# Loading the first norm's scales alone, splitting the first weight loads, and moving one more projection ahead of the first norm in a streaming encoder step

## The chip, the cores and the metric

The kernel runs on one core of one Trainium2 chip. The metric is the device time of one execution in microseconds. The times before are those of three runs: 1094.95, 1096.83 and 1100.05 us, so the median is 1096.83 us. One execution was profiled apart; it took 1095.87 us and its recorded span is 1093.7 us.

## The reference, cut to what matters

One layer of a hybrid encoder works on 576 rows of width 1024: 512 rows of a prompt and 64 rows of a sample. The two are independent sequences with their own states; they share the weights.

```python
def _trunk(x, mem_k, mem_v, conv_a_prev, s_gdn, s_gla, ffn_prev, p):
    y, c_new, sa, sb = _mixer(_rmsnorm(x, p['norm_mix'][l]), p, l, ...)
    x = x + y
    x = x + _cross_attn(_rmsnorm(x, p['norm_mem'][l]), mem_k[l], mem_v[l], ...)
    f, f_new = _conv_ffn(_rmsnorm(x, p['norm_ffn'][l]), p['w_up'][l], ...)
    x = x + f
    return _rmsnorm(x, p['norm_final']), ...
```

`_mixer` projects the normalised rows to q, k and v of a gated delta rule (four heads, after a causal convolution of width 4), to q, k and v of a gated linear attention, to their gates and to two merge gates; both recurrences run in chunks of 64. `_conv_ffn` projects up to 2 x 2816 columns, convolves them causally (width 3), multiplies SiLU of one half with the other and projects down. Everything is float32; the states and the last rows before each convolution are outputs too.

## The kernel before, in words

The rows lie transposed: eight tiles `x[k]` of 128 features by 576 rows. Each float32 operand of a large product is split in a rounded part and a remainder (`xh`, `xl`; a weight tile gives `wh`, `wl`), and a product is the sum of three matmuls: `wh`·`xh`, `wh`·`xl`, `wl`·`xh`. One weight tile of 128 output columns (1024 floats per partition) makes two PSUM accumulators, of 256 and 320 rows: 48 matmuls. In a trace the weight loads are `wr<-wt` (on the queue of SyncE, SP), the split is two ACT instructions, and the remainder of most tiles is finished by a second load from DRAM that adds (`w<-wt`, issued by GpSimd, POOL).

The norm does not come first. The scale of the norm over features (`g`) is put into `xh`/`xl` by `norm_prep`, and the factor of each row (`rbc`) is applied when a PSUM result is taken out. So the projections start as soon as the first rows and weights are there, and the sums of squares (`ssq` in `c_rstat`), the reciprocal root (on POOL) and the broadcast of the factor (two `dg` tiles against ones) are worked out beside them.

What sets the order. All engine work is recorded by a planner, the class `Driver`. A main generator, `main`, yields the large projections tile by tile; smaller generators, called chains (convolutions, gates, the recurrences, the norms), are advanced between its pieces. The planner has a cost for each instruction and a time at which each tile is written; when a chain yields, its next piece may be put into TensorE's order only `MARGIN` us of planned time after its inputs are planned to be ready (`advance`, and `drain` where the main generator must wait). Instructions of ACT, DVE, POOL and SP come into their queues in the order of their planned starts. Each engine works its queue strictly in order, so an instruction that waits holds up everything behind it on that engine.

The beginning (lines 703 to 717 and `main` from line 1648): the loads of the vector table `vec` (276 columns), then alternately a tile of `x` and a piece of 512 columns of the first two weight tiles; on ACT and DVE the splits in the same order; then 96 matmuls for q and k of head 0 (`first2`). Behind these stand the sums of squares (20 small matmuls, `sm<-keep,acc` and `sm<-keep,sq`), 16 small products of `x` with the 32 columns of the low-rank gate (`sm<-x,w`), and then v of head 0. Its accumulators are taken out when the row factor is there; the chain `c_first` does that for q and k and starts the gates. The `HEADS` list then gives the order of the other projections, qb (the linear attention's q) next.

Further back: the merge gates (`gate_finish`, product form `run_product`) follow the recurrences; then `mem_prep` loads the sample's last rows of the ConvFFN (`fst`, DMA `fst<-st_ffn`) and the memory tokens (`mem`), whose squares are summed on POOL into `macc`; then eight `out` tiles. In the ConvFFN each of the 44 column tiles `fu` gets four small POOL instructions: a zero for the two columns ahead of the prompt, a copy of two columns from `fst` ahead of the sample, and two copies into `fout`.

Of the kernel before, what the change touches and what calls it, by code (L numbers as in the profile page):

```python
# [34 lines left out]
BACK = 6.0  # L35
MARGIN = 0.6
LAG = 0.0
NWARM = 18

# [221 lines left out]
class Driver:  # L261
# [7 lines left out]
    def __init__(self, pe, sync):  # L269
        self.pe, self.sync = pe, sync  # L270
        self.chains = []
        self.done = set()
        self.now = 0.0
        self.half = self.mode = None
        self.last = 0.0
        self.wrote = {}
# [185 lines left out]
    def drain(self, until):  # L462
        while not until():
            r = self.step(MARGIN)
            if r is None:
# [16 lines left out]
def tile_trunk(ctx, tc, xT, memT, wt, wd, vec, cst, w0, wgate, st_gdn, st_conv, st_gla, st_ffn, ckT, cv,  # L482
# [220 lines left out]
    cst_t = tp.tile([P, NM - 256], F32, tag="cst", name="cst", bufs=1)  # L703
    DMA(vec_t, vec)
    x = []
# [33 lines left out]
    V.tensor_scalar(onh, vcol(C_ONA, 2), 0.5, None, op0=ALU.mult)  # L739
    fst = cp.tile([P, 2 * NJ, 2], F32, name="fst")  # L740
    fout = cp.tile([P, 2 * NJ, 4], F32, name="fout")
# [67 lines left out]
    def ssq(accs, t, n, ps):  # L809

        for i, (acc, o) in enumerate(accs):
            PE.matmul(ps[0:n, t:t + 1], acc[:, o + t * 128:o + t * 128 + n], ones[:, 0:1], start=i == 0, stop=i == len(accs) - 1)

    def pads(t_):
# [827 lines left out]
    def main():  # L1642
# [4 lines left out]

        def wpart(i, k):
            c = slice(512 * k, 512 * k + 512)
            wh, wl = wready[i]  # L1650
# [25 lines left out]
        V.tensor_tensor(r4(w0_t, 32), r4(w0_t, 32), vcol(C_GMIX, 8).unsqueeze(2).broadcast_to([P, 8, 32]), op=ALU.mult)  # L1676
# [7 lines left out]
        drop(*(t_[:] for t_ in raws))  # L1684
        emit_weight(2)
        DMA(wg_t, wgate)
# [49 lines left out]
        for kd, i in HEADS:  # L1736
# [4 lines left out]
            elif kd == "qb":  # L1741
                drv.spawn(c_gla(i))
            b = b0
            if i > 0 or kd not in ("q", "k", "v"):
                b = []
# [68 lines left out]
        for pair, prod in product_order(GPAIRS):  # L1814
# [198 lines left out]
        def kept(col, u):  # L2013
            G.tensor_copy(fout[:, col, 0:2], u[:, 512:514])
            G.tensor_copy(fout[:, col, 2:4], u[:, 578:580])

# [3 lines left out]
        def scaled(j, col, u):  # L2020
            X.tensor_tensor(u[:, 2:582], u[:, 2:582], N["n3"][1][:, 0:580], op=ALU.mult)
            G.tensor_copy(u[:, 514:516], fst[:, col, :])
            kept(col, u)

        def up_finish(pair, prod, a, b, c):
            j = pair[0][1]
            if prod == "P1":
                ups[j] = slot("fu"), slot("fu")
                for u in ups[j]:
                    G.memset(u[:, 0:2], 0.0)  # L2030
            ug, uv = ups[j]
# [253 lines left out]
    def mem_prep():  # L2285
        DMA(fst, st_ffn)
        mxs = []
# [137 lines left out]
```

## Time and profile before

| what | us | where |
|---|---|---|
| median of three runs | 1096.83 | the times |
| profiled execution, its own time | 1095.87 | the times |
| span of that execution | 1093.7 | page |
| TensorE busy | 1081.5 | page, part 1 |
| DVE, ACT, POOL busy | 740.1, 707.9, 328.1 | page, part 1 |
| TensorE's share of the chain that ended last | 95% | page, part 4 |
| first large matmul | 6.65 | timeline |

A busy TensorE in this profile is not TensorE at its peak: matmuls overlap and their ends are modelled, so what a stretch is worth is read from the starts of its matmuls. Two groups of tile names matter: `bank` are the accumulators of the large products, `sm` those of the chains. The granted clock in the windows view is a share of full speed; records of it begin only 10.2 us into the span, so an earlier window shows 1.00 whatever it was.

### The profile page before, as it was taken

The numbers are of one execution on the slowest core, as the hardware profiler recorded it, in microseconds if no ns is written. First come the engines' busy times: TensorE is split into PE (matmuls) and PEld (weight loads), VectorE is DVE, ScalarE is ACT, GpSimd is POOL, SyncE is SP. The second block draws the span as 40 slices with busy tenths as digits, with TensorE's granted clock in tenths as the row PEclk, the third lists the DMA queues.
The fourth block names the chain that finished last, engine by engine and source line by source line (L and its number), as shares of the span: only waits on it lengthen the run. The fifth ranks groups of instructions, "written<-read, shape, count | busy, mean of one in ns | idle before, by whom it ended". The sixth has DMA issues, their size and how long they took to land.

```text
span 1093.7 us, 21490 instructions
## 1 busy us (share of the span) xinstructions
PE 1081.5 (99%) x8259; PEld 1048.5 (96%) x8259; DVE 740.1 (68%) x1446; ACT 707.9 (65%) x1385; POOL 328.1 (30%) x608
## 2 busy tenths in 40 slices
PE   9999999999999999999999999999999999999997
PEld 8999989998988999999999999999999999999997
DVE  6675647666676767977736768577796776676634
ACT  7766446754766786466756668866786675767643
POOL 2333014421432324022111122444443433434320
PEclk9999999999999999999999999999999999999999
DMA  8675235743556899488884359766887886787863
GB/s 266 135 174 121 39 82 119 182 100 88 124 112 148 196 231 221 170 226 203 226 211 129 70 125 228 176 148 125 187 185 184 178 201 147 181 190 168 171 120 111
DMA packets 67094, 174.88 MB, mean 160 GB/s; under 512 B 7664, under 2 KB 13168, under 8 KB 66992
## 3 DMA queue, kind: packets, MB, share of 16 engines
q0 software_dynamic: 30528, 73.41, 39.0%
q1 hardware_dynamic: 36464, 100.10, 28.7%
q8 instruction: 65, 1.06, 0.4%
q14 instruction: 37, 0.30, 0.1%
HBM read 159.99 MB, written 5.37 MB: 151 GB/s over the span
## 4 chain that ended last, share of the span: by engine, by line
PE 95%; DMA 2%; issue 2%; POOL 0%; ACT 0%; DVE 0%; DVEq 0%; POOLq 0%; SPq 0%
PE bank L292 65%; PE sm L292 30%; DMA wr<-wt 1%; DMA w<-ws 1%; DMA w<-wt 1%; POOL w L292 0%; ACT w L292 0%; DVE ws L292 0%; DVEq L2415 0%; POOL rtf L292 0%; SPq L292 0%; POOLq L2415 0%; ACT vb L292 0%; DVE rin L292 0%; POOLq L292 0%
## 5 line engine op out<-in xcount | busy, mean ns | idle before, releaser
L292 PE MATMUL bank<-xh,w 128*128 128x320 f32 (+3 forms) x1824 | 349.2, 303 | 1.8 <-ACT w L292 1.6
L292 PEld LDWEIGHTS bank<-xh,w 128*128 128x128 f32 x1824 | 279.2, 190 | 6.9 <-ACT w L292 1.7
L292 PE MATMUL bank<-ach,w 128*128 128x288 f32 (+3 forms) x1320 | 255.7, 296 | 1.2 <-DMA w<-ws 1.1
L292 POOL DMA_DIRECT2D w<-wt x149 | 131.5, 886 | 374.1 <-ACT w L292 319.3
L292 PEld LDWEIGHTS bank<-ach,w 128*128 128x128 f32 x1320 | 207.5, 188 | 2.6 <-DMA w<-ws 1.6
L292 PE MATMUL bank<-xl,w 128*128 128x256 f32 (+3 forms) x912 | 204.4, 296 | 0.0
L292 ACT CAST w<-wr 128x512 fp32r<-128x512 f32 (+2 forms) x201 | 158.3, 790 | 25.1 <-PE bank L292 14.8
L292 ACT ACTIVATE w<-wr 128x512 fp32r<-128x512 f32 (+2 forms) x181 | 142.8, 790 | 40.3 <-PE bank L292 29.3
L292 PE MATMUL bank<-acl,w 128*128 128x288 f32 (+3 forms) x660 | 159.2, 295 | 0.0
L292 PEld LDWEIGHTS bank<-xl,w 128*128 128x128 f32 x912 | 156.0, 190 | 0.0
L292 PE MATMUL sm<-ach,w 128*128 128x290 f32 (+1 forms) x576 | 124.6, 296 | 0.1
L292 PEld LDWEIGHTS bank<-acl,w 128*128 128x128 f32 x660 | 116.7, 188 | 0.0
L292 PEld LDWEIGHTS sm<-ach,w 128*128 128x128 f32 x576 | 95.7, 189 | 0.3 <-ACT kvh L292 0.3
L292 ACT CAST w<-ws 128x512 fp32r<-128x512 f32 x124 | 74.3, 615 | 26.5 <-DVE ws L292 17.4
L292 PE MATMUL sm<-acl,w 128*128 128x290 f32 (+1 forms) x288 | 79.1, 296 | 0.0
L292 DVE SCALAR_TENSOR_TENSOR fc<-fu,vec,fc 128x578 f32<-128x578 f32 x88 | 72.1, 829 | 9.7 <-ACT fc L292 9.5
L292 DVE TENSOR_TENSOR w<-ws,w 128x512 fp32r<-128x512 f32 x92 | 63.0, 688 | 16.7 <-ACT w L292 15.2
L292 DVE TENSOR_TENSOR x<-x,bank 128x256 f32<-128x256 f32 (+1 forms) x78 | 31.9, 443 | 38.9 <-PE bank L292 38.9
L292 PEld LDWEIGHTS sm<-acl,w 128*128 128x128 f32 x288 | 54.3, 189 | 0.0
L292 ACT ACTIVATE fc<-fu,vec 128x578 f32<-128x578 f32 x44 | 38.2, 871 | 24.1 <-POOL fu L292 24.0
L292 POOL DMA_DIRECT2D w<-wd x32 | 27.6, 873 | 82.7 <-ACT w L292 80.5
L292 PE MATMUL bank<-oh,w 128*128 128x256 f32 (+1 forms) x256 | 44.9, 295 | 0.3 <-DMA w<-wt 0.3
(381 smaller groups left out, 2008.0 us busy)
## 6 DMA issues: line engine op xcount, KB each, us to landing
wr<-wt SPq DMA_DIRECT2D x134, 512.0 KB, 5.7
w<-wt POOLq DMA_DIRECT2D x56, 512.0 KB, 7.3
w<-wt POOLq DMA_DIRECT2D x93, 256.0 KB, 6.0
wr<-wd SPq DMA_DIRECT2D x24, 384.0 KB, 4.1
w<-wd POOLq DMA_DIRECT2D x24, 384.0 KB, 6.6
w<-ws POOLq DMA_DIRECT2D x31, 256.0 KB, 4.6
x<-xT SPq DMA_DIRECT2D x16, 288.0 KB, 3.8
y<-xT SPq DMA_DIRECT2D x8, 288.0 KB, 4.3
```

The lines of the kernel that those rows point to most:

```text
L292: fn(*args, **kw)
```

## The change

It has five parts.

1. The eight columns of the first norm's scales are loaded alone in front; the other 268 columns of `vec` follow after the fourth `x` tile. What reads those other columns at the beginning (`ea` on ACT, `onh` on DVE) stands later in its queue.
2. The first two weight tiles are loaded and split in pieces of 256, 256 and 512 columns each (`FIRST`) in place of 512 and 512. The third weight tile is loaded and split earlier (`emit_weight(2)` before the squares).
3. The sums of squares of the first norm and the small products of `x` are placed by the planner inside v of head 0 and no longer ahead of it, and qb's first tile goes ahead of the wait for the first norm: q, k, v and qb, four tiles. The accumulators of q and k are taken out by ACT or DVE, whichever is planned to be free sooner (`moved`); it becomes DVE.
4. The chain margin is 0.3 up to the end of the merge gates and 0.6 behind (`drv.margin`).
5. `fst` is allocated late, with four columns per tile, the first two of them zero, so that one strided copy replaces the zero and the copy ahead of the sample, and one strided copy replaces the two into `fout` (`ends`).

```diff
-MARGIN = 0.6
+MARGIN = 0.3, 0.6
+FIRST = [(0, slice(0, 256)), (1, slice(0, 256)), (0, slice(256, 512)), (1, slice(256, 512)), (0, slice(512, 1024)), (1, slice(512, 1024))]
...
-            c[0] = self.last + MARGIN
+            c[0] = self.last + self.margin
         elif isinstance(r, list):
-            c[0] = self.ready_at(*r) + MARGIN
+            c[0] = self.ready_at(*r) + self.margin
...
-    DMA(vec_t, vec)
+    DMA(vec_t[:, C_GMIX:C_GMIX + KT], vec[:, C_GMIX:C_GMIX + KT])
...
-        if k < 4:
-            c = slice(512 * (k // 2), 512 * (k // 2) + 512)
-            DMA(raws[k % 2][:, c], wt[k % 2][:, c])
+        if k < 6:
+            a, c = FIRST[k]
+            DMA(raws[a][:, c], wt[a][:, c])
+        if k == 3:
+            DMA(vec_t[:, C_GMIX + KT:NV], vec[:, C_GMIX + KT:NV])
...
+    def apart(t_, a, b, n):
+
+        o = t_[:, a:a + n]
+        return bass.AP(tensor=o.tensor, offset=o.offset, ap=[tuple(o.ap[0]), (b - a, 2), (1, n)])
...
         for o, i in zip(two(u, True, 3, 518), pv(ps, True)):
-            A.copy(o, i)
+            moved(o, i)
...
-        xprep(0)
-        wpart(0, 0)
-        xprep(1)
-        wpart(1, 0)
-        xprep(2)
-        wpart(0, 1)
-        xprep(3)
-        wpart(1, 1)
-        for k in range(4, 8):
+        for k in range(KT):
             xprep(k)
+            if k < 6:
+                wpart(k)
+        emit_weight(2)
         sqs = [sq_act(k) for k in range(KT)]
...
-        drv.spawn(c_rstat("n1", [(acc, 0), (sqs[7], 0)], 4, True, 0.0), 2)
-        pa, pb_ = sm(), sm()
-        for o, c in ((pa[:, 0:256], slice(0, 256)), (pb_[:, 0:320], slice(256, T))):
-            for k in range(KT):
-                g = 32 * (k % 4)
-                PE.matmul(o[g:g + 32, :], w0_t[:, 32 * k:32 * k + 32], x[k][:, c], start=k < 4, stop=k >= 4)
-        yield
+        drv.spawn(c_rstat("n1", [(acc, 0), (sqs[7], 0)], 4, True, 0.0))
 
         def c_first():
+            yield [w0_t]
+            pa, pb_ = sm(), sm()
...
         yield from tile_proj("v", 0, xs, b0)
+        b1 = []
+        yield from tile_proj("qb", 0, xs, b1)
         yield ("first",)
...
+        drv.margin = MARGIN[1]
         wops, merged = {}, {}
...
-            G.memset(u[:, 0:2], 0.0)
...
-            G.tensor_copy(u[:, 514:516], fst[:, col, :])
-            kept(col, u)
+            ends(col, u)
             return u
...
+        def ends(col, u):
+            G.tensor_copy(apart(u, 0, 514, 2), fst[:, col, :].rearrange("p (a b) -> p a b", b=2))
+            G.tensor_copy(fout[:, col, :].rearrange("p (a b) -> p a b", b=2), apart(u, 512, 578, 2))
...
     def mem_prep():
-        DMA(fst, st_ffn)
+        nonlocal fst
+        fst = fp.tile([P, 2 * NJ, 4], F32, tag="fst", name="fst", bufs=1)
+        G.memset(fst, 0.0)
+        DMA(fst[:, :, 2:4], st_ffn)
```

Where the instructions stand. The first loads on SP's queue, before:

```order
L292 DMA vec<-vec 128x276
L292 DMA x_82<-xT 128x576
L292 DMA wr_80<-wt 128x512
L292 DMA x_83<-xT 128x576
L292 DMA wr_81<-wt 128x512
L292 DMA x_84<-xT 128x576
```

and in the changed kernel:

```order
L294 DMA vec<-vec 128x8
L294 DMA x_82<-xT 128x576
L294 DMA wr_80<-wt 128x256
L294 DMA x_83<-xT 128x576
L294 DMA wr_81<-wt 128x256
L294 DMA x_84<-xT 128x576
```

The order of tiles is the same; the table ahead of them shrinks to 8 columns and each weight piece to half.

TensorE's order behind the last matmuls of k of head 0 (`w_110` holds its remainder; `bank_337` is an accumulator of v, `sm_257` the sums, `sm_295` the small products; the ten rows of each small group read alike but for the names of their tiles), before:

```order
L292 MATMUL bank_155<-xh_125,w_110 128x256
L292 MATMUL bank_156<-xh_125,w_110 128x320
L292 MATMUL sm_257<-keep,acc_106 128x1
...
L292 MATMUL sm_257<-keep,sq_133 64x1
L292 MATMUL sm_295<-x_82,w_90 32x256
...
L292 MATMUL sm_296<-x_89,w_90 32x320
L292 MATMUL bank_337<-xh_111,w_135 128x256
```

and in the changed kernel (v is `bank_263`, the sums `sm_330`, the small products `sm_271` and `sm_272`):

```order
L294 MATMUL bank_147<-xh_124,w_109 128x320
L294 MATMUL bank_263<-xh_110,w_127 128x256
L294 MATMUL bank_264<-xh_110,w_127 128x320
L294 MATMUL bank_263<-xl_111,w_127 128x256
L294 MATMUL bank_264<-xl_111,w_127 128x320
L294 MATMUL sm_271<-x_82,w_90 32x256
...
L294 MATMUL sm_272<-x_89,w_90 32x320
L294 MATMUL bank_263<-xh_112,w_127 128x256
...
L294 MATMUL bank_264<-xl_115,w_127 128x320
L294 MATMUL sm_330<-keep,acc_105 128x1
```

Four matmuls of v now stand ahead of the small products, and eight more ahead of the sums. The first `bank_263` needs the accumulator of q to be taken out, since only four `bank` tiles exist.

The load of the ConvFFN's rows on SP's queue, before:

```order
L292 DMA wr_5121<-wt 128x1024
L292 DMA fst<-st_ffn 128x88
L292 DMA mem_5142<-memT 128x512
L292 DMA mem_5146<-memT 128x512
L292 DMA mem_5151<-memT 128x512
```

and in the changed kernel:

```order
L294 DMA wr_5135<-wt 128x1024
L294 DMA fst<-st_ffn 128x44x2
L294 DMA mem_5157<-memT 128x512
L294 DMA mem_5161<-memT 128x512
L294 DMA mem_5166<-memT 128x512
```

On POOL's queue of the changed kernel, where the zeroing that this load waits for stands:

```order
L294 DMA w_4972<-wt 128x512
L294 DMA w_5011<-wt 128x1024
L294 MEMSET fst 128x176
L294 DMA w_5070<-wt 128x1024
L294 DMA w_5102<-wt 128x1024
L294 DMA w_5137<-wt 128x1024
```

The load's place among the others is the same, but it now writes 44 runs of two floats per partition in place of one run of 88, and waits for a POOL instruction that stands behind the issue of a weight's adding load.

More of the change, by code (lines that the diff above doesn't have):

```diff
@@ L275, in __init__ @@
         self.last = 0.0
+        self.margin = MARGIN[0]
         self.wrote = {}
@@ L463, in drain @@
         while not until():
-            r = self.step(MARGIN)
+            r = self.step(self.margin)
             if r is None:
@@ L812, in ssq @@
             PE.matmul(ps[0:n, t:t + 1], acc[:, o + t * 128:o + t * 128 + n], ones[:, 0:1], start=i == 0, stop=i == len(accs) - 1)
+    fst = None
+    def apart(t_, a, b, n):
+        o = t_[:, a:a + n]
+        return bass.AP(tensor=o.tensor, offset=o.offset, ap=[tuple(o.ap[0]), (b - a, 2), (1, n)])
     def pads(t_):
@@ L1646, in main, with wpart @@
             wready[i] = (w_tile()[:], w_tile()[:])
-        def wpart(i, k):
-            c = slice(512 * k, 512 * k + 512)
+        def wpart(k):
+            i, c = FIRST[k]
             wh, wl = wready[i]
@@ L1697, in main @@
         raw_u = [conv_raw(ps) for ps, _, _ in first2]
-        drv.spawn(c_rstat("n1", [(acc, 0), (sqs[7], 0)], 4, True, 0.0), 2)
-        pa, pb_ = sm(), sm()
-        for o, c in ((pa[:, 0:256], slice(0, 256)), (pb_[:, 0:320], slice(256, T))):
-            for k in range(KT):
-                g = 32 * (k % 4)
-                PE.matmul(o[g:g + 32, :], w0_t[:, 32 * k:32 * k + 32], x[k][:, c], start=k < 4, stop=k >= 4)
-        yield
-        def c_first():
+        drv.spawn(c_rstat("n1", [(acc, 0), (sqs[7], 0)], 4, True, 0.0))
+        def c_first():
+            yield [w0_t]
+            pa, pb_ = sm(), sm()
+            for o, c in ((pa[:, 0:256], slice(0, 256)), (pb_[:, 0:320], slice(256, T))):
+                for k in range(KT):
+                    g = 32 * (k % 4)
+                    PE.matmul(o[g:g + 32, :], w0_t[:, 32 * k:32 * k + 32], x[k][:, c], start=k < 4, stop=k >= 4)
             while not drv.ready("n1"):
@@ L1742, in main @@
                 drv.spawn(c_gla(i))
-            b = b0
-            if i > 0 or kd not in ("q", "k", "v"):
+            b = b1 if kd == "qb" else b0
+            if i > 0 or kd not in ("q", "k", "v", "qb"):
                 b = []
@@ L2021, in scaled @@
             X.tensor_tensor(u[:, 2:582], u[:, 2:582], N["n3"][1][:, 0:580], op=ALU.mult)
-            G.tensor_copy(u[:, 514:516], fst[:, col, :])
-            kept(col, u)
+            ends(col, u)
         def up_finish(pair, prod, a, b, c):
```

7 lines of the change are left out of this document (removed).

## The prediction

> **What bounds the kernel now.** I read the page first, then the waits of TensorE, then the chain and the windows, and last the timeline at the two places where the change touches the supply. The page says that TensorE is the bound: busy share, the chain by engine, and all its waits over the whole run.
>
> ```profile
> PE 1081.5 (99%) x8259; PEld 1048.5 (96%) x8259; DVE 740.1 (68%) x1446; ACT 707.9 (65%) x1385; POOL 328.1 (30%) x608
> ...
> PE 95%; DMA 2%; issue 2%; POOL 0%; ACT 0%; DVE 0%; DVEq 0%; POOLq 0%; SPq 0%
> ...
> PE bank L292 <- ACT w L292: 1.6, 1, 1.6
> PE bank L292 <- DMA w<-ws: 1.1, 1, 1.1
> PE warm L292 <- POOL mhalf L292: 1.0, 1, 1.0
> PE bank L292 <- DMA w<-wt: 0.3, 1, 0.3
> PE bank L292 <- ACT vb L292: 0.2, 1, 0.2
> ```
>
> The last five rows are total, count and longest: five waits, 4.2 us in sum, the first of them the start itself. So no rearrangement can win more than these waits and whatever the clock gives back. 0.5% of the time, 5.5 us, is about the least that can be told from no change, and it is more than all five waits together.
>
> The clock is the other item. The chain of waits at the front (start, length, what) and the windows (busy time and instructions of PE, PEld, DVE, ACT, POOL, then granted clock, DMA share, GB/s):
>
> ```profile
> 1.66 4.30 DMA wr<-wt
> ...
> 5.98 0.63 ACT w L292
> ...
> 6.65 14.59 PE bank L292 x96
> ...
> 34.66 12.82 PE bank L292 x96
> ```
>
> ```profile
> 6.83:10.24 3.41, 3.41 (x15) 3.41 (x16) 2.73 (x4) 2.74 (x5) 0.00 (x0) 1.00 1.04 403
> 10.25:13.66 3.41, 3.41 (x27) 3.41 (x26) 3.41 (x6) 3.30 (x5) 0.00 (x0) 1.00 1.06 406
> ...
> 23.90:27.31 3.41, 3.41 (x27) 1.55 (x20) 2.29 (x6) 0.29 (x1) 2.74 (x5) 0.50 1.05 245
> ```
>
> The first 96 large matmuls took 14.59 us, the same number at 34.66 took 12.82: 1.77 us lost. The windows say where: 15 matmuls up to 10.24 and 27 in as long a stretch behind, so TensorE ran at half speed until 10.24 (no clock record is there that early). From 23.90 to 27.31 it was granted 0.50 once more: half of 3.41 us, 1.7 us lost.
>
> **The front: an earlier start, and the clock behind it.** The timeline of ACT and of TensorE:
>
> ```profile
> 2.99 0.20 ACT L292 ACTIVATE ea<-vec 128x4 f32<-128x4 f32 x1 [0.97 <-DMA vec<-vec]
> 4.17 0.77 ACT L292 ACTIVATE xh<-x,vec 128x576 fp32r<-128x576 f32 x1 [0.97 <-DMA x<-xT]
> 5.98 0.62 ACT L292 CAST w<-wr 128x512 fp32r<-128x512 f32 x1 [1.03 <-DMA wr<-wt]
> ```
>
> ```profile
> 1.00 4.10 PE L292 MATMUL warm<-onesr 128*128 128x128 f32 x18 [1.00 <-POOL mhalf L292]
> 6.65 0.85 PE L292 MATMUL bank<-xh,w 128*128 128x256 f32 x2 [1.55 <-ACT w L292]
> ```
>
> Ahead of the first matmul lie 138 KB of table, 288 of `x` and 256 of weights. The change takes 134 and 128 KB away, 262 KB; at the 403 GB/s of the window at 6.83 that is 0.65 us. The CAST of 512 columns took 0.62; ACT's row for 1024 columns, quoted further down, took 1.04, so 256 columns come to 0.41, 0.2 us less. So the first matmul comes about 0.85 us earlier, at 5.8, if nothing else is late: `ea` leaves ACT's front, and `xh` of 0.77 fits ahead of the weights.
>
> What 0.85 us are worth depends on the clock. If the full clock comes at 10.24 again, they are spent at half speed: 0.4 us. If it follows the start, 0.85. If the pause of 1.55 us between the warming matmuls and the first real one was what kept the window up to 6.83 from counting, a pause of 0.7 may let it count, and full speed comes a window earlier: 0.85, and of the 1.77 lost only what runs up to 6.83, half of 1 us, stays: 0.85 + 1.25 = 2.1. I take **−1.0**, near the middle one, bounds −0.4 and −2.1.
>
> [...]
>
> **The second half-speed window.** It follows on these rows of TensorE, the first and the last group of the sums and the small products:
>
> ```profile
> 21.08 0.31 PE L292 MATMUL sm<-keep,acc 128*128 128x1 f32 x2
> ...
> 23.02 0.26 PE L292 MATMUL sm<-keep,sq 128*64 128x1 f32 x2
> 23.21 3.45 PE L292 MATMUL sm<-x,w 128*32 128x256 f32 x32
> ```
>
> Twenty matmuls of one column fill 2.2 us of the window before 23.90, and then the clock is halved. The small products lie in that stretch and take 3.45 us. Now the sums stand inside v of head 0, twelve large matmuls later and with the small products ahead of them. [...]
>
> **New waits in the front.** Before, sums and small products (2.2 + 3.45 us) stood between k and v and gave three things time: the accumulators' take-out, the squares, and v's weights. Their rows:
>
> ```profile
> 20.90 1.40 ACT L292 COPY u<-bank 128x256 f32<-128x256 f32 x6
> ...
> 19.01 1.04 ACT L292 ACTIVATE w<-wr 128x1024 fp32r<-128x1024 f32 x1
> ```
>
> ```profile
> 18.56 2.39 DVE L292 TENSOR_TENSOR acc<-acc,sq 128x576 f32<-128x576 f32 x2 [0.39 <-ACT sq L292]
> ```
>
> That cover is gone. v's first matmul needs q's accumulators, now taken out by DVE behind an addition of about 0.75; half of the six copies is 0.7 us, while k's last six matmuls give 0.8: a wait of 0 to 0.8. v's weights (two rows of 1.04) now stand ahead of six squares on ACT: not late. The squares end some 2.1 us later in exchange, and DVE's last addition, which ended at 20.95, follows them and the six copies: 23 to 24.5. The sums are due near 23.4 (21.08, less 1.0, plus 1.7 for the small products at full speed and 1.6 for twelve large matmuls): 0 to 1.2 late. Together 0 to 2.0; I take **+0.6**, as the planner places them by the time at which their input is planned.
>
> qb ahead of the wait for the norm adds no matmul. It covers root, broadcast and take-out (23.4 to about 30 before, in which TensorE had v): 0.
>
> **The halved margin.** The chain of waits from 60 to 380 alternates between large products and chains:
>
> ```profile
> 231 pieces in order of time: start us, us, what
> ```
>
> So about 115 chain pieces stand in that stretch, and of all waits there only the 0.2 on `vb` is a chain's. Moving a piece 0.3 us earlier gains nothing on a TensorE that has no gap, and costs where the inputs are later than planned. Below: 0. Above: one piece in ten losing its full 0.3 us, 115 × 0.1 × 0.3 = 3.4. One 0.2 us wait at the margin of 0.6 says that plans are good: **+0.2**.
>
> **Where the lead is spent.** A TensorE that is half a microsecond ahead reaches the stretches that wait for weights. The chain there, with the DMA share of the windows:
>
> ```profile
> 321.45 7.30 DMA w<-ws
> ...
> 328.79 2.93 PE bank L292 x20
> ```
>
> ```profile
> 380.00:405.00 25.00, 24.91 (x188) 24.68 (x186) 16.98 (x30) 20.97 (x36) 6.90 (x8) 1.00 0.94 220
> 405.00:430.00 25.00, 24.72 (x187) 24.49 (x187) 17.03 (x38) 17.31 (x31) 10.07 (x12) 1.00 1.00 256
> ```
>
> The wait of 1.1 at 328.79 is a reload for a late piece; with another order of chains it may vanish (−1.1) or grow by the lead (+1). From 380 to 430 the DMA engines are full and the adding loads come just in time (0.3 wait): a lead of a microsecond may be lost there. Net **0**, bounds −1.1 and +1.0.
>
> **The ConvFFN's rows.** In the FFN the change takes 44 zeros away and makes one copy of each two. POOL's group of zeros (shortest, median, longest in ns):
>
> ```profile
> L292 POOL MEMSET fu<- x44: 89/436/940, 689.7 to 1022.0; 128x2 f32 x44
> ```
>
> 44 × 0.44 is 19 us of a POOL that is 30% busy and absent from the waits of TensorE behind the start: 0. The load is the risk. The places on SP, POOL and TensorE before, and between them two DMA groups (KB, us from issue to landing) of the first `mem` and of the load issued at 417.81:
>
> ```profile
> 393.33 0.43 SPq L292 DMA_DIRECT2D fst<-st_ffn  x1
> 393.81 7.82 SPq L292 DMA_DIRECT2D mem<-memT  x4
> ```
>
> ```profile
> 399.01 0.86 POOL L292 DMA_DIRECT2D w<-wt  x1 [5.44 <-ACT w L292]
> ...
> 411.25 6.19 POOL L292 TENSOR_TENSOR macc<-macc,msq 128x256 f32<-128x256 f32 x7 [1.29 <-ACT msq L292]
> 417.81 0.90 POOL L292 DMA_DIRECT2D w<-wt  x1 [0.37 <-issue]
> ```
>
> ```profile
> mem<-memT SPq DMA_DIRECT2D x1, 256.0 KB, 7.9
> ```
>
> ```profile
> w<-wt POOLq DMA_DIRECT2D x1, 512.0 KB, 7.8
> ```
>
> ```profile
> 431.51 0.44 PE L292 MATMUL bank<-oh,w 128*128 128x256 f32 x2
> ```
>
> The zeroing of `fst` stands behind POOL's issue at 399.01, so SP is held from 393.3 to about 400. The four `mem` issues behind it last to 401.6 anyway: four of 0.45 from 400.3 end at 402.1, half a microsecond late. Then the load itself: 128 × 44 runs of 8 bytes in place of 128 rows, 352 for each of 16 engines. The nearest row with small packets, a window of 0.3 us (packets, MB, share of 16 engines):
>
> ```profile
> q1 hardware_dynamic: 143, 0.04, 53.7%
> ```
>
> These are 288-byte packets, nine for each engine in 0.3 us: 18 ns of an engine's work or 33 ns of time each, so 6.3 to 11.8 us for 352. `mem`, behind it on the queue, landed at 393.8 + 7.9 = 401.7; its squares on ACT feed the seven additions on POOL from 411.25, some 8 us of slack with the work between taken off. Behind the additions stands the adding load issued at 417.81, landed at 425.6, used at 431.51: 5.9 us more. Delay 7 to 12 against 14: no stall at these prices, 5 us if a run costs half as much again. Between 8 and 14 ACT stands at `mem` with the splits of weights behind it, which is why nothing is not taken. **+0.3**, bounds 0 and +5.
>
> [...] The 288-byte packets are the smallest that the trace shows; a price for 8 bytes none has.
>
> **Sum.** −1.0 − 0.7 + 0.6 + 0.2 + 0 + 0 + 0.3 = **−0.6 us**, on the profiled execution's own 1095.87 (span 1093.7 and 2.2 around it). That execution lies 0.96 below the median of 1096.83, so the median goes to **1096.2**.
>
> **The rivals.**
> *The clock gives all back.* Full speed a window earlier, no second half-speed window, and the wait at 328.79 gone: −2.1 − 1.7 − 1.1, with no new wait, −4.9: 1091.9. For it: the shorter pause before the first matmul. Against: the twenty sums stay together, and TensorE has less cover. 0.15.
> *The supply takes the lead.* The front wins what I say or more, and TensorE arrives at the full DMA engines from 380 to 430 earlier and waits for it: no change, 1096.8. For it: shares of 0.94 and 1.00, and the 0.3 us wait. Against: a slack of 5.9 at 431.51 shows that not all loads are late. 0.13.
> *The 8-byte runs.* One mechanism, at 393 to 432: SP held by the zeroing, the runs ahead of `mem` and the next weights, POOL's additions late, and with them the adding load behind. Slower by 5: 1101.8. It decides from a delay of 14 us, that is, 352 runs at over 38 ns. 0.11.
> *The margin.* Plans 0.3 us too optimistic in one piece of ten: +3.4 − 0.8 for the rest = +2.6: 1099.4. Against: the single 0.2 us wait. 0.08.
>
> **How the numbers follow.** The forecast has 0.53, its own range 1093.5 to 1098.5. Faster by over 0.5% (below 1091.3) takes something under half of the first rival and a little of the forecast's unknowns: 0.08. Slower by over 0.5% (above 1102.3) takes less than half of the runs' rival and a rest for several waits at once: 0.07. Within: 0.85. The range reaches from the clock's rival to just below that of the runs: 1091.8 to 1100.8.
>
> **What would show it.** The first large matmul near 5.8 and a chain row for the first 96 of 14.0 to 14.6 (13.4 if the clock comes early); a granted 0.50 once, or not, before 30 us; q's accumulators waited for less than 0.8 us ahead of v; no wait of TensorE between 60 and 310 over 0.5; `fst` landing within 20 us of its issue, and the large product near 431 without a wait. The forecast is wrong if TensorE's waits grow by over 3 us in sum, or if the two half-speed stretches both go.

## The result and the profile after

The changed kernel takes 1104.30 us in the median of six runs (1102.1 to 1109.84), the kernel before 1096.18 in six (1094.95 to 1100.05): a ratio of 1.0084, 95% interval 1.0063 to 1.0104. It is slower by 8 to 9 us, and the prediction (1096.2, range 1091.8 to 1100.8) was wrong. The profiled execution took 1108.24 us, span 1106.5, which is 3.9 us over the median: it is one of the three longer of the six, which were granted 0.991 to 0.993 of the clock in the mean, where the three shorter (1102.1 to 1103.03) were granted 0.996 or 0.997.

The page of the changed kernel, and all waits of its TensorE (total, count, longest):

```profile
PE 1087.3 (98%) x8259; PEld 1051.8 (95%) x8259; DVE 737.8 (67%) x1449; ACT 705.7 (64%) x1384; POOL 320.7 (29%) x523
...
PE 89%; DMA 5%; issue 2%; ACT 2%; DVE 1%; POOL 1%; DVEq 0%; POOLq 0%; SPq 0%; ACTq 0%
```

```profile
PE bank L294 <- DVE gt L294: 2.2, 2, 1.4
PE sm L294 <- ACT os L294: 1.8, 1, 1.8
PE bank L294 <- ACT w L294: 1.6, 1, 1.6
PE bank L294 <- DMA w<-wt: 1.0, 2, 0.8
PE sm L294 <- DMA w<-ws: 1.0, 2, 0.8
PE warm L294 <- POOL onesr L294: 1.0, 1, 1.0
PE sm L294 <- DVE R L294: 1.0, 1, 1.0
PE sm L294 <- ACT Y L294: 0.7, 1, 0.7
PE bank L294 <- DMA w<-ws: 0.4, 1, 0.4
PE sm L294 <- DVE xi L294: 0.3, 1, 0.3
PE sm L294 <- DMA w<-wt: 0.2, 1, 0.2
```

Before there were five waits and only one of 0.2 us belonged to a chain. Now TensorE waits for four chain pieces (`os`, `R`, `Y`, `xi`), 3.8 us in sum. All its waits together grew from 4.2 to 11.2 us, the span by 12.8, so the list of waits alone does not show where the time went. (That the waits grow by over 3 us was what the prediction had named as a sign against it.) Counting TensorE's matmuls from the first and comparing the starts in both traces does: the 2100th starts 1.6 us later than before (at 264), the 2250th 8.3, the 2850th 6.9, the 3300th 10.5 (at 432), the 3900th 12.0, the last 12.7. Two places, then: 264 to 290, and 370 to 490. The chain of waits at the first, and the window behind it:

```profile
265.56 2.92 PE sm L294 x22
268.48 0.02 issue
268.50 0.68 ACT ach L294
269.18 0.59 ACT zt L294
269.77 0.02 issue
269.79 0.77 DVE z L294
...
270.59 0.38 ACT os L294
...
271.00 7.61 PE sm L294 x34
```

```profile
270.59 0.37 ACT L294 COPY os<-sm 64x256 f32<-64x256 f32 x1 [0.83 <-DVE z L294]
```

```profile
271.40:278.30 6.90, 6.90 (x31) 4.66 (x31) 0.00 (x0) 1.26 (x2) 0.00 (x0) 0.51 0.00 0
```

TensorE stood 1.8 us for a copy (`os`) that stands third on ACT, behind a gate's operand (`ach`) and the activation `zt`; and between `zt` and `os` ACT itself was idle for 0.83 us, until DVE had finished `z`. Behind the wait the clock was granted at 0.51 for 6.9 us, two windows: 34 short matmuls took 7.61 us.

At the front the first large matmul came at 6.67 and not at 5.8. ACT's timeline:

```profile
4.25 1.28 ACT L294 ACT_TABLE_LOAD   x1 [4.25 <-DMA x<-xT]
5.55 0.77 ACT L294 ACTIVATE xh<-x,vec 128x576 fp32r<-128x576 f32 x1
6.23 0.39 ACT L294 CAST w<-wr 128x256 fp32r<-128x256 f32 x1
```

The load of ACT's table now waits for the first `x` tile. Before, it ran at 0.74 with `ea` behind it, and `x` was there at 4.17. So the saved bytes did not bring `x` earlier; the first weights were there when ACT came to them, where it had waited 1.03 us for them before, but 1.28 us of table load stood in the place of that wait.

The clock was later, too. In this execution it was recorded as full from 12.04 on, in the one before from 10.24. The matmuls around that point, in the view of the windows:

```profile
8.62:12.03 3.41, 3.41 (x16) 3.41 (x16) 3.27 (x7) 3.02 (x7) 0.00 (x0) 1.00 1.05 390
12.04:15.45 3.41, 3.41 (x28) 3.41 (x28) 3.11 (x5) 3.16 (x6) 0.00 (x0) 1.00 1.03 401
```

So the 96th large matmul started 0.8 us later than before, though the first started at the same time. The edit need not have done that: in the six profiles whose front is unaltered, the record of the full clock begins anywhere from 9.98 to 11.91.

The second place holds the load of the ConvFFN's rows. POOL, TensorE and SP there:

```profile
427.64 6.13 POOL L294 TENSOR_TENSOR macc<-macc,msq 128x256 f32<-128x256 f32 x7 [9.37 <-ACT msq L294]
```

```profile
428.22 0.42 PE L294 MATMUL bank<-oh,w 128*128 128x320 f32 x1 [1.35 <-DVE gt L294]
```

```profile
409.47 0.70 SPq L294 DMA_DIRECT2D fst<-st_ffn  x1
410.23 12.21 SPq L294 DMA_DIRECT2D mem<-memT  x4
```

### The profile page after: what moved, and what is told of

Same layout as the page of the kernel before. It is cut to its first block, busy times and chain, and to the rows that moved or that the text cites. A ratio compares the mean times of both kernels' runs of the same rounds, so it can differ in the third digit from the quotient of the medians.

```text
span 1106.5 us, 21413 instructions
## 1 busy us (share of the span) xinstructions
PE 1087.3 (98%) x8259; PEld 1051.8 (95%) x8259; DVE 737.8 (67%) x1449; ACT 705.7 (64%) x1384; POOL 320.7 (29%) x523
## 4 chain that ended last, share of the span: by engine, by line
PE 89%; DMA 5%; issue 2%; ACT 2%; DVE 1%; POOL 1%; DVEq 0%; POOLq 0%; SPq 0%; ACTq 0%
PE bank L294 60%; PE sm L294 28%; DMA w<-ws 2%; DMA mem<-memT 1%; DMA w<-wt 1%; ACT w L294 1%; DMA wr<-wt 1%; POOL w L294 0%; DMA x<-xT 0%; ACT mh L294 0%; DVE w L294 0%; DVE ws L294 0%; POOL macc L294 0%; ACT msq L294 0%; DVE z L294 0%
## 5 line engine op out<-in xcount | busy, mean ns | idle before, releaser
L294 PE MATMUL bank<-xl,w 128*128 128x256 f32 (+3 forms) x916 | 206.7, 298 | 0.0
L294 ACT CAST w<-wr 128x512 fp32r<-128x512 f32 (+3 forms) x203 | 158.5, 783 | 27.1 <-PE bank L294 11.6
L294 DVE TENSOR_TENSOR w<-ws,w 128x512 fp32r<-128x512 f32 x91 | 62.3, 688 | 16.8 <-ACT w L294 14.0
```

The source lines that it names most:

```text
L294: fn(*args, **kw)
```

## The experiments

The word *margin* always means the margin up to the gates; behind them it stays 0.6. Ratios are against the kernel before on the same chip; a ratio is not the quotient of the two medians, so a small one can differ from what a median suggests. The values of the margin differ from run to run, and the changed kernel with 0.6 was not run.

**Margin, rows and table load, one at a time in the changed kernel, and the margin alone in the kernel before.**

```diff
-MARGIN = 0.3, 0.6
+MARGIN = 0.4, 0.6
```

> The changed kernel with a chain margin of 0.4 in place of 0.3 up to the gates; nothing else is edited. Theory A (the halved margin puts chain pieces into TensorE's order before their inputs are there, and the 2.8 us of waits near 268 and 285, with the half clock behind them, are its price): the waits shrink by a third or go, and the time falls to 1098 to 1101. Theory B (qb's tile ahead of the first norm starts the chains some 8 us later against the large products, so that cover runs out near 265 whatever the margin): a stall of over 1 us stays between 255 and 295 and the time stays at 1103 to 1106.

Measured: 1105.37 us, ratio 1.0075 (1.0060 to 1.0090). The stall was not gone, it stood elsewhere: 3.42 us for `xi` at 205, with the clock at half from 204.4 to 211.3, and nothing at 270. That speaks against A.

```diff
 # the kernel before
-MARGIN = 0.6
+MARGIN = 0.35, 0.6
```

> The kernel before with a chain margin of 0.35 up to the gates, nothing else changed: the margin alone, nearly the whole of that part. Theory A: waits of TensorE on chain pieces of 2 to 4 us in sum between 60 and 310 and 1100 to 1103. Theory B: waits under 0.5 us there and 1096 to 1097.

Measured: 1099.06 us, ratio 1.0012 (0.9998 to 1.0027). Between 60 and 310 TensorE waited for one piece only, as before:

```profile
PE bank L293 <- ACT vb L293: 0.2, 1, 0.2
```

Of the few microseconds that the margin was priced at, none came as a chain wait there. At 395 TensorE waited 0.89 us for the take-out `gt`, as it did in the changed kernel at 403 (0.86). For this kernel A falls as it stood.

```diff
-        fst = fp.tile([P, 2 * NJ, 4], F32, tag="fst", name="fst", bufs=1)
-        G.memset(fst, 0.0)
-        DMA(fst[:, :, 2:4], st_ffn)
+        DMA(fst, st_ffn)
...
+            G.memset(u[:, 0:2], 0.0)
+            G.tensor_copy(u[:, 514:516], fst[:, col, :])
```

> The changed kernel with the ConvFFN's rows loaded as before: one run of 88 floats per partition, no zeroing on POOL ahead of it, four small POOL instructions for each column tile again. Theory C (the 8-byte runs and the zeroing delay the memory tokens by 8 us, ACT and POOL stand behind them and the adding loads come late): the 3.5 us lost between 377 and 478 fall to 1 or less and the time to 1101. Theory D (that loss belongs to the full DMA engines, which TensorE meets with other phases): under 1 us changes, 1103.5 to 1105.

Measured: 1105.14 us, ratio 1.0078 (1.0054 to 1.0103): nothing gained. The second place lost nearly as much, 4.7 us between the 2850th and the 3900th matmul, where the changed kernel lost 5.1. The wait for `gt` at 428 was gone, and a wait of 1.2 us for an adding load stood at 413 in its place. That is the number which theory D had named (under 1 us changes). This profile says more about the first place: the same waits of TensorE (1.82 and 0.98, and 0.67 ahead of them at 248), but the clock stayed:

```profile
271.40:278.30 6.90, 6.83 (x51) 4.88 (x52) 1.76 (x4) 1.65 (x5) 0.00 (x0) 1.00 0.11 13
```

51 matmuls in the window where the changed kernel had 31.

```diff
+        early = cp.tile([P, KT], F32, name="early")
+        A.activation(early, vec_t[:, C_GMIX:C_GMIX + KT], AF.Identity)
         for k in range(KT):
             xprep(k)
```

> The changed kernel with one small activation of the eight scales in front on ACT, so that the load of ACT's table (1.28 us at 4.25, behind the wait for the first x tile) runs while x is under way. First large matmul at 5.4 in place of 6.67. If the front's gain was eaten by that load alone: 0.6 to 1.3 us less, 1103.0 to 1103.7. If the clock comes a window earlier as well: 1102. If the planner's other order or phase decides: a change of over 2 us of either sign, and of its place behind 200 us.

Measured: 1103.35 us, ratio 1.0049 (1.0032 to 1.0065). The first matmul came even earlier than had been predicted for the change:

```profile
0.74 1.28 ACT L294 ACT_TABLE_LOAD   x1 [0.74 <-PEq L2418]
2.39 0.21 ACT L294 ACTIVATE early<-vec 128x8 f32<-128x8 f32 x1 [0.37 <-DMA vec<-vec]
4.09 0.77 ACT L294 ACTIVATE xh<-x,vec 128x576 fp32r<-128x576 f32 x1 [1.49 <-DMA x<-xT]
4.77 0.39 ACT L294 CAST w<-wr 128x256 fp32r<-128x256 f32 x1
...
6.55 0.78 ACT L294 ACTIVATE xh<-x,vec 128x576 fp32r<-128x576 f32 x1 [1.38 <-DMA x<-xT]
```

```profile
5.21 0.85 PE L294 MATMUL bank<-xh,w 128*128 128x256 f32 x2
```

1.46 us earlier at the start, but the second `x` tile came only at 6.5, and by the 50th matmul 0.4 us were left. And again the same waits near 270, now with three half-speed windows behind them:

```profile
271.20:281.40 10.20, 10.20 (x45) 7.10 (x45) 1.68 (x3) 1.63 (x3) 0.00 (x0) 0.50 0.08 21
```

**The order undone, whole or in part, and the other parts alone.**

```diff
-        b1 = []
-        yield from tile_proj("qb", 0, xs, b1)
         yield ("first",)
...
+MARGIN = 0.55, 0.6
```

> The changed kernel with qb's tile back behind the wait for the first norm, and a chain margin of 0.55 up to the gates; the sums and small products stay inside v, front and ConvFFN rows as changed. Theory B (qb ahead starts the chains late): no chain wait of over 0.5 us between 90 and 300, no half clock there, and 1096 to 1099. Theory B' (the sums inside v, or the planner's new order as such): a chain wait of over 1 us somewhere between 90 and 300 and 1101 to 1106.

Measured: 1096.44 us, ratio 1.0011 (0.9989 to 1.0032). The longest chain wait was 0.74 us at 110, none near 270. All of the loss is given back, though two things were changed at once. At 72 TensorE waited 1.76 us for the take-out `u`, as it did by 1.2 to 1.8 us in all six kernels without qb ahead but with the sums inside v; this kernel is not slower for all that.

```diff
-        drv.spawn(c_rstat("n1", [(acc, 0), (sqs[7], 0)], 4, True, 0.0))
+        drv.spawn(c_rstat("n1", [(acc, 0), (sqs[7], 0)], 4, True, 0.0), 2)
+        pa, pb_ = sm(), sm()
...
-        yield from tile_proj("qb", 0, xs, b1)
...
+MARGIN = 0.4, 0.6
```

> The changed kernel with its third part undone (sums, small products and qb where they were, accumulators taken out by ACT) and a chain margin of 0.4 up to the gates; front and ConvFFN rows as changed. Theories B and B': no chain wait of over 0.5 us between 90 and 300; 1096 to 1099. If the front's other order or the margin makes the stalls: 1102 to 1106.

Measured: 1100.12 us, ratio 1.0024 (1.0005 to 1.0043). No chain wait over 0.24 us. Most of what is left comes from the front: of the 4.7 us that this profile lost, 3.2 were lost by the 500th matmul. TensorE waited 1.78 us at 23.0 for the sums' input `acc`, since the split of the third weight stands ahead of the squares, and here no v covers it.

```diff
 # the kernel before
-    DMA(vec_t, vec)
+    DMA(vec_t[:, C_GMIX:C_GMIX + KT], vec[:, C_GMIX:C_GMIX + KT])
...
+            if k < 6:
+                wpart(k)
+        emit_weight(2)
```

> The kernel before with the front alone changed: the scales loaded alone, weights in pieces of 256, the third weight tile split ahead of the squares, the other columns of the table later. Margin, order of the sums, qb and the ConvFFN's rows as before. ACT's table load is then behind the first x tile, so the first large matmul stays near 6.6 and the time within 1 us of the kernel before, 1096 to 1098.5. If the front itself costs: over 1099.

Measured: 1098.16 us, ratio 1.0012 (0.9998 to 1.0027), with the same wait:

```profile
23.32 0.38 PE L294 MATMUL sm<-keep,acc 128*128 128x1 f32 x2 [1.34 <-DVE acc L294]
```

```diff
 # the kernel before
+        fst = fp.tile([P, 2 * NJ, 4], F32, tag="fst", name="fst", bufs=1)
+        G.memset(fst, 0.0)
+        DMA(fst[:, :, 2:4], st_ffn)
```

> The kernel before with the ConvFFN's rows as changed and nothing else. Theory C (zeroing and 8-byte runs delay the memory tokens and what stands behind them): 2 to 4 us lost between 377 and 478, 1099 to 1101. Theory D (no cost of its own): under 1 us, 1096 to 1098.

Measured: 1096.27 us, ratio 0.9994 (0.9980 to 1.0008). TensorE's wait is there, but it is small; the 1.1 us that this profile lost between the 2850th and the 3900th matmul do not show in the median:

```profile
417.03 0.42 PE L292 MATMUL bank<-oh,w 128*128 128x320 f32 x1 [1.02 <-DVE gt L292]
```

**Which part of the order.**

```diff
 # the kernel before
         yield from tile_proj("v", 0, xs, b0)
+        b1 = []
+        yield from tile_proj("qb", 0, xs, b1)
         yield ("first",)
```

> The kernel before with qb's tile ahead of the wait for the first norm and nothing else changed (the margin stays 0.6). Theory B (one more tile ahead puts the chains later against the large products): one or more chain waits of over 0.5 us between 90 and 300, more if they bring a half-clock window, and 1099 to 1105. If qb ahead does harm only together with the sums inside v: no such wait and 1096 to 1098.

Measured: 1097.10 us, ratio 1.0005 (0.9991 to 1.0019). qb ahead by itself costs nothing. But it did not make the norm late here either: the broadcast of the row factor stood at 27.0, and at 28.1 in the kernel before, whose profile has a half-speed window ahead of it where this one has none. In both TensorE has 104 large matmuls ahead of the broadcast.

```diff
 # the changed kernel without qb ahead
-MARGIN = 0.55, 0.6
+MARGIN = 0.35, 0.6
```

> As the experiment without qb ahead, with a margin of 0.35 in place of 0.55. Margin harmless by itself: 1096 to 1098, no chain wait over 0.7 us before 300. Margin costs: the wait of 0.8 to 0.9 us for a gate (gt) near 400 that every run with a margin of 0.4 or less showed and none above, and stalls at chain pieces before 300 in addition: 1099 to 1102.

Measured: 1101.25 us, ratio 1.0040 (1.0024 to 1.0057). Waits of 1.15, 0.41 and 0.94 us between 279 and 287.

```diff
 # on that, in c_first
+            drv.done.add("first")
+            yield 4.0
             for a in range(2):
                 drv.spawn(c_conv(a, 4 * a, *conv_head(None, 4 * a, raw_u[a])))
-            drv.done.add("first")
```

> As the run with margin 0.35 and without qb ahead, but the first chains (convolutions and gates) are held back by 4 us of planned time after the first norm, while the large products go on. Theory B: what hurts is the lateness, so stalls at chain pieces appear as with qb ahead, and it is 3 us or more slower than its neighbour. If it is something else about qb's tile (its accumulators, its buffers): within 1.5 us of its neighbour.

Measured: 1100.79 us, ratio 1.0039 (1.0023 to 1.0056): no slower than its neighbour. The third convolution did start 4.5 us later (44.7 in place of 40.2), the broadcast stayed at 34.3. Later convolutions alone do no harm.

```diff
 # e5 with
+        A.activation(early, vec_t[:, C_GMIX:C_GMIX + KT], AF.Identity)
```

> As the experiment without qb ahead at margin 0.55, with the small activation in front that lets ACT's table load run early. First large matmul at 5.4 in place of 6.5: 0.5 to 1.2 us faster than that run, 1095.2 to 1096, a little faster than the kernel before (ratio 0.998 to 0.9995). If the lead is spent on other waits: no difference, 1096.5.

Measured: 1098.03 us, ratio 1.0007 (0.9993 to 1.0021). Against its neighbour the lead of 1.1 us at the start was still 0.9 at 370. It was gone behind 373, where TensorE waited 1.17 us for an adding load, and at 419 two waits for `gt` (1.88 and 0.56) put this kernel 3.0 behind.

```diff
-MARGIN = 0.3, 0.6
+MARGIN = 0.52, 0.6
```

> The changed kernel with a chain margin of 0.52 up to the gates and nothing else edited. If the margin, in the changed order, is what stalls TensorE: no chain wait of over 0.8 us between 200 and 300, no half clock there, no wait for a gate near 400, and 1097 to 1100. If qb ahead together with the sums inside v does it, whatever the margin: a stall of over 1 us again, 1102 to 1106.

Measured: 1103.42 us, ratio 1.0053 (1.0033 to 1.0073). No wait near 270, but one of 3.64 us at 105. The ratio is lower than at 0.3, by intervals that overlap.

```diff
-MARGIN = 0.3, 0.6
+MARGIN = 0.45, 0.6
```

> The same with 0.45. By the margin: between the runs at 0.4 and 0.52, with a wait at a chain piece of some tenths of a microsecond, 1099 to 1104. By the order: 1102 to 1106.

Measured: 1104.62 us, ratio 1.0063 (1.0039 to 1.0088). 5.13 us for `on` at 376, with two half-speed windows. Four margins in the changed order, four places:

```profile
205.29 1.12 PE L294 MATMUL sm<-keep,c 128*128 128x128 f32 x4 [3.42 <-DVE xi L294]
```

```profile
375.68 0.68 PE L294 MATMUL sm<-keep,on 64*128 64x64 f32 x4 [5.13 <-DVE on L294]
```

```profile
104.82 0.71 PE L294 MATMUL sm<-bd,yc 128*128 128x128 f32 x4 [3.64 <-ACT yc L294]
```

```diff
 # e12 with the rows as before
-        DMA(fst[:, :, 2:4], st_ffn)
+        DMA(fst, st_ffn)
```

> The run without qb ahead, margin 0.55 and the early table load, with the ConvFFN's rows loaded as before. That run waited 1.9 us for a gate tile at 419, behind remainders of the late memory tokens on DVE. If the 8-byte runs make them late: that wait is gone, the time 1.5 to 2.5 us under its 1098.0, about 1096. If it is the full DMA engines: the same time within 1 us and a wait near 400 to 430 of another kind.

Measured: 1097.35 us, ratio 0.9987 (0.9972 to 1.0001). The wait for `gt` is gone. It ran beside other runs of the kernel before than its neighbour did; by the two ratios the rows cost 0.2%, and the intervals overlap.

```diff
 # on that
-MARGIN = 0.55, 0.6
+MARGIN = 0.65, 0.6
```

> The same with a margin of 0.65. If waits at chain pieces still cost at 0.55 (0.7 us at 110): 0.5 to 1 us less, 1095. If a larger margin only puts the chains later: the same or up to 2 us more.

Measured: 1101.77 us, ratio 1.0034 (1.0021 to 1.0048). A larger margin is worse, by intervals that lie apart: two waits at 270 and 274, 2.3 us.

```diff
 # the kernel before
+        yield from tile_proj("qb", 0, xs, b1)
...
+MARGIN = 0.4, 0.6
```

> The kernel before with qb ahead of the wait for the first norm and a margin of 0.4 up to the gates; sums, front and ConvFFN rows as before. If both edits of the order are needed: no chain wait over 0.5 us between 60 and 480, 1096.5 to 1099 (ratio up to 1.002). If qb ahead with a low margin is enough: a stall of over 1 us and 1101 to 1105.

Measured: 1096.19 us, ratio 0.9995 (0.9985 to 1.0004). qb ahead and a low margin together are free as long as the sums stand where they were.

```diff
 # the kernel before, with the third part and
+MARGIN = 0.33, 0.6
```

> The third part (sums and small products inside v, qb ahead, take-out by ACT or DVE) with a margin of 0.33 up to the gates, and nothing else: the front and the ConvFFN's rows as before. If the order makes the loss: a stall of over 1.4 us at a chain piece between 60 and 480 and 1101.5 to 1106, ratio 1.004 to 1.009. If the front's or the rows' edit is needed for it: 1096 to 1099.

Measured: 1097.77 us, ratio 1.0013 (0.9999 to 1.0027), and no chain wait at all between 60 and 480. So the order does not make the loss without the rest either. With the old front the sums are ready earlier (TensorE takes them from 21.9, against 25.7) and the broadcast is at 31.0.

**What the twenty profiles have in common.** All chains start from the broadcast of the first norm's factor. What goes with the ratios is how many large matmuls TensorE has ahead of it. The chain of the kernel before and that of the changed kernel, from the small products and the sums up to the broadcast (the last `sm` row), and the broadcast itself:

```profile
26.66 1.58 PE bank L292 x8
28.23 0.80 PE sm L292 x4
```

```profile
28.07 0.96 PE L292 MATMUL sm<-dg,onesr 128*128 128x512 f32 x4
```

```profile
27.90 8.61 PE bank L294 x52
36.52 0.80 PE sm L294 x4
```

```profile
36.35 0.97 PE L294 MATMUL sm<-dg,onesr 128*128 128x512 f32 x4
```

Before, 96 matmuls of q and k and 8 of v stand ahead; in the changed kernel 96, all 48 of v and 16 of qb. The counts in all traces:

| large matmuls ahead | kernels | broadcast at, us | longest wait of an `sm` tile from 60 to 400, us | ratio |
|---|---|---|---|---|
| 104 | before; margin 0.35; rows; qb ahead, margin 0.6 and 0.4; front; old order | 26.8 to 31.6 | 0 to 0.68 | 0.9994 to 1.0024 |
| 124 | order alone | 31.0 | 0 | 1.0013 |
| 144 | without qb: margin 0.55, also with the table load and with old rows; 0.65; 0.35, also with later chains | 31.3 to 34.5 | 0.73 to 1.39 | 0.9987 to 1.0040 |
| 160 | all changes: 0.3, 0.4, 0.45, 0.52, old rows, table load | 34.3 to 36.7 | 1.8 to 5.1 | 1.0049 to 1.0084 |

The time of the broadcast is the weaker sign, since it also holds the half-speed window that one execution has near 30 and another has not: two kernels of the third row without such a window are at 31.3 and 32.1, the four with one at 33.0 to 34.5.

Two things can be said of the parts. qb ahead, on top of the others, costs 0.35 to 0.44% at either margin: 1.0075 and 1.0084 against 1.0040 near 0.35, and 1.0053 against 1.0011 near 0.55, with intervals that just lie apart. And no part alone costs over 0.15% by its ratio: the front (1.0012) and the order with its margin (1.0013) come to 0.25%, both with the rows as before to 0.78%.

It is a relation of twenty profiles and not a mechanism that was isolated: why a later place of the broadcast gathers stalls at 105, 205, 270 or 376 is not shown, and the one run that held the convolutions back by hand did not get slower. Of the theories, A falls as stated, since the stall moved and did not shrink at four margins. The margin is not without effect, though: without qb ahead it is 1.0040 at 0.35 and 1.0007 at 0.55 (there with the table load early) on the same chip, by intervals that just lie apart, and 1.0034 at 0.65 against 0.9987 at 0.55. B, chains that start late, stands as this relation only. C was right in its mechanism and small in its price. D had the number right, with the one wait of 1.2 us for an adding load for it.

## Why the prediction was wrong, by its steps

- **Earlier start (−1.0): failed.** The step was "if nothing else is late: `ea` leaves ACT's front". The table load ahead of the first activation was late: 1.28 us behind the wait for `x`. With a small activation ahead, the first matmul came at 5.21 (predicted 5.8), but the run was not clearly faster, since the second `x` tile was late next. The sum priced one arrival and not the one behind it. Of the three cases for the clock none came: the record of the full clock begins at 12.04, and among like fronts it moves by 1.9 us.
- **Second half-speed window (−0.7): not gained.** It stood from 29.1 to 32.5. No run shows a term of this size. Of the twenty profiles 13 have such a window between 20 and 36 and 7 none, the unaltered order on both sides: the margin alone and the rows alone had none, the kernel before had one. The edit does not decide it.
- **New waits in the front (+0.6): mechanism right, other kernels.** In the changed kernel v covered the late sums. Where they stood ahead of v, TensorE waited 1.34 and 1.78 for `acc`. The last addition ended at 25.5 and not at 23 to 24.5.
- **qb ahead (0): the step that failed most.** "It covers root, broadcast and take-out" is true of the covering. What was left out is what stands behind it in TensorE's order: the broadcast, whose operands DVE had ready at 31.4, was run at 36.35 behind all of v and 16 matmuls of qb, 8.3 us later than before, and all chains with it. On top of the other parts that was worth 0.35 to 0.44%, some 4 to 5 us, where 0 was priced. It needed the late sums as well: they came 4.6 us later (25.74 in place of 21.08), with the split of the third weight (two rows of 1.04) ahead of six of the squares, an edit which I had costed for `acc` alone, and with 12 matmuls of v and the small products ahead of them; under the same edit of the order, but with the old front, they come at 21.85. qb alone, in the kernel before, changes neither the place of the broadcast nor the time. How the later start becomes stalls stays open.
- **The halved margin (+0.2, up to 3.4): the waits came, the cause was another.** The rival said one piece in ten loses its 0.3 us. Three pieces lost 0.7 to 1.8 us each, and the margin of 0.52 lost 3.64 at one. The waits are several times the margin, so 0.3 us of it can't be what each of them lacks. In the kernel before, a margin of 0.35 cost 0.12% with an interval down to nothing. With the other parts a margin of 0.3 to 0.35 cost some 0.3% (about 3 us) against 0.52 to 0.55, near the upper end of the price and not by its mechanism: each margin gives another order, and 0.65 was no better.
- **What a wait costs: mis-sized.** Each bound of the sum took a wait at its length. The same two waits (1.82 and 0.98, 2.8 us) cost 3.8 us between the 2100th and the 2250th matmul where the clock stayed full, 6.7 with two half-speed windows behind the first and 8.1 with three. These executions took 1104.32, 1108.24 and 1108.35 us. The 3.4 us named as the margin rival's upper end were about the right length of waiting, at about half its price in the profiled execution.
- **The ConvFFN's rows (+0.3, up to 5): mechanism right, price small.** SP was held until POOL's zeroing, 7.2 us, `mem` came late, ACT and POOL stood behind it (POOL idle 9.37 us before its additions). `fst` took 14.9 us to land where it took 8.0, the first `mem` 15.8 in place of 7.9. But not the adding load was late next: DVE stood at the remainder `ml` of `mem` with the take-out `gt` behind it, and TensorE waited 1.0 to 1.9 us there for its accumulator in five of the eleven profiles with the new rows. Alone the edit cost nothing that can be measured (0.9994). One reading of the prediction is wrong: packets of 288 bytes are not the smallest that the trace before shows. It has 128 of 144 bytes from 15.8 to 17.2, at 14 ns of an engine each, so the 18 ns for each run were too many.
- **The lead (0).** There was none to spend. The kernel with an early table load and without qb ahead had one of 1.1 and lost it at 373 in a wait for an adding load, just ahead of the stretch in which the supply's rival had put the loss.

The forecast's likeliest case rested on adding the parts, each within 1 us. Alone, each part was measured within 1.5 us of nothing by its ratio, so the terms were not far off for parts on their own; together they were, by 8 to 9 us, since qb ahead and the margin cost in the changed kernel what they do not cost in the kernel before.

## What to carry to other kernels

Where a planner writes the order, parts that are free alone can add up: look at what they do to the one result from which the following work starts, and at what stands ahead of it in the bounding engine's queue. On an engine that is busy for 99%, a wait among short matmuls is to be priced with the half-speed windows that may follow: here 2.8 us of waiting cost 3.8, 6.7 or 8.1. And when the first activation of a kernel changes, see where its table load goes: here its 1.28 us went from 0.74 to 4.25, behind the wait for `x`.

## What the hardware showed beside

**Windows of half speed differ between runs of like waits.** Apart from the one at the very end of the span, their lengths are multiples of 3.41 us in every profile (3.4 at 23.9 in the kernel before, 6.8 at 271.4 in the changed kernel, 10.2 at 271.2 with the early table load), at phases that differ from run to run. A stop of 1.8 us near 271 was followed by none, two or three. Waits of 1.56, 1.88 and 1.98 us among large products, near 382, 419 and 384, were followed by none. One of 3.64 came with one, one of 3.42 and one of 5.13 with two.

**A DVE instruction beside one of POOL.** In the kernel with a margin of 0.52 the wait of 3.64 us has this behind it:

```profile
101.42 2.43 DVE L294 TENSOR_TENSOR dec<-dec,cst 128x512 f32<-128x512 f32 x1
```

```profile
101.57 3.58 POOL L294 TENSOR_TENSOR qgp<-qb,e 64x576 f32<-64x576 f32 x2
```

```profile
L294 DVE TENSOR_TENSOR dec<-dec,cst x5: 416/692/2431, 78.3 to 293.5; 128x512 f32<-128x512 f32 x4, 64x256 f32<-64x256 f32 x1
```

The same instruction takes 0.69 in the median and took 2.43 while POOL's product ran; at margins of 0.4 and 0.45 it was 2.47 and 2.46 beside the same product, without a chain wait of over 0.52 us behind it. The 1.74 us more are about as long as the first of POOL's two products (1.72). Why it took longer is not shown: DVE's row starts 0.15 us ahead of POOL's, and running beside each other is not enough. In the kernel with 0.45 the same two overlap once more at 220.73, with DVE 0.20 us ahead, and there DVE's took 0.69; in the changed kernel DVE's `kg<-kb,e` at 219.34 took its usual 0.75 beside POOL's `rr<-l,mhalf` (1.68 from 218.98). The wait of 1.8 near 271 in the changed kernel has no such pair in it: there a copy stood third on ACT. At the places looked at the stalls thus have different causes, and why they gather where the chains start late is left open.

**Small runs.** 5632 runs of 8 bytes took 8.3 to 14.9 us to land, in ten of eleven profiles over 11.5, where the same 44 KB in 128 rows took 6.4 to 8.1 in nine. In the changed kernel's trace such a packet holds an engine for 9.8 ns in the mean, 3.4 us for an engine's 352, so the estimate of 6.3 to 11.8 us was too high. The first `mem`, next on the queue, landed after 10.0 to 16.8 us in place of 6.4 to 8.6.

No kernel tried was clearly faster than the kernel before: the fastest ratios, 0.9987 (0.9972 to 1.0001) and 0.9994 (0.9980 to 1.0008), include no change.
